# Starting every tile that the tensor engine reads at a multiple of 128 bytes in a two-layer decoder trunk

## The chip, the cores and the metric

The kernel runs as one program on one core of a Trainium2 chip. The metric is the device time of an execution in microseconds (us). Before the change it is 2058.88 us, the median of three runs (2056.41 to 2058.89).

## What is computed

Two decoder layers on 512 tokens of width 1024, all in float32. Layer 0 mixes tokens by attention (8 stick-breaking heads, 8 dilated heads), layer 1 by an mLSTM (8 heads). Each layer has a SwiGLU feed-forward network (FFN) of width 2816 ahead of its mixer and another behind it.

```python
def _rms_norm(x, g):
    y = x * lax.rsqrt(jnp.mean(x * x, axis=-1, keepdims=True) + EPS)
    return y * g

def _swiglu(x, w_gate, w_up, w_down):
    return (jax.nn.silu(x @ w_gate) * (x @ w_up)) @ w_down

for layer in range(2):
    x = x + 0.5 * _rms_norm(_swiglu(_rms_norm(x, g[0]), *ffn[layer, 0]), g[1])
    mix = attention(_rms_norm(x, g[2])) if layer == 0 else mlstm(_rms_norm(x, g[2]))
    x = x + _rms_norm(mix, g[3])
    x = x + 0.5 * _rms_norm(_swiglu(_rms_norm(x, g[4]), *ffn[layer, 1]), g[5])
```

## The kernel before

**Products in three passes.** A float32 operand is split into a high part (a cast to `fp32r`, `hi`) and a low part (the rest, `lo`), and a product is the sum of three matmuls: hi by hi, hi by lo, lo by hi (`mm3`, and the loops of `products`, `ffn` and `out_part`). All go through `mm` (L72), so the profile shows most matmuls under that one line, and they are told apart by their tiles. In a name such as `pg<-xnh,whi` the tile behind the arrow, `xnh`, is the moving operand, whose columns stream through the array, and the last one, `whi`, is the stationary operand, loaded into the array as weights beforehand (PEld in the profile).

**Stages.** Six run one after the other: FFN, attention, FFN, FFN, mLSTM, FFN. `proj` multiplies the normalized activations `xnh`/`xnl` (8 blocks of 128 features by 512 tokens) by 128 columns of a weight matrix: 8 blocks by three passes make 24 matmuls of 512 columns, or, at the start of a stage, where the tokens come in two halves, 48 of 256 columns. Weights come by DMA into `raw`, ACT casts them to `whi`, DVE (POOL for the first of a stage) subtracts to get `wlo` (`chunk`). The FFN's down-projection is a Strassen-like scheme: `left` and `right` form sums of activation and weight blocks, `hop` and `wop` split them into `hhi`/`hlo` (stationary) and `dhi`/`dlo` (moving, 512 columns), and `products` and the end of `ffn` accumulate into the banks `pc` and `po`. The mixers' `values` stream weights against stationary activations (`pv<-whi,xnh`, 256 columns), their heads multiply small tiles (`z`, `pv`, `nb`, `sb`), and `out_part` and `down` project the result (`po<-whi,mhi`, moving `whi`, stationary `mhi`/`mlo`).

**Order.** The order of the work is written in the program: a generator per head or token block gets its turn by an estimate of PE's clock (`clk`, `spawn`, `tick`). Each engine then runs its instructions in the order in which they were written.

**Where tiles start.** A pool lays its tiles out one behind the other in each partition, each rounded up to 32 bytes. `ident` starts at byte 2176 (17 times 128) and takes 512 bytes, `mhalf` (4 bytes, L52) takes 32, and so `x` and all that lies behind it start 32 bytes past a multiple of 128, until the next small tile shifts the rest again. In the built program the start, as the rest of a division by 128, is:

| tiles | read by PE as | start before | start after |
|---|---|---|---|
| `ident` | moving | 0 | 0 |
| `xnh`, `xnl` | moving in `pg`, `pq`, `ob`; stationary in `pv` | 32 | 0 |
| `whi`, `wlo` of the main pool | stationary in `pg`, `pq`, `ob`; moving in `pv`, `po` | 32 | 0 |
| `whi`, `wlo` of the pool `xp` (first 4 weight tiles of the second and the fourth FFN) | stationary in `pg` | 96 | 0 |
| `hhi`, `hlo`; `dhi`, `dlo` | stationary; moving, in `pc` and `po` | 64; 64 | 0; 0 |
| `mhi`, `mlo` | stationary in `po` | 64 | 0 |
| `tri` | stationary in `z` | 64 | 0 |
| heads' tiles (`ks`, `qq`, `ql`, `p5hi`, `p5lo`, `vt`, `qhi`, `khi`, `vhi`, `wshi`, `qshi`, `ones`, ...) | both, in `z`, `pv`, `nb`, `sb` | 96 | 0 |

The rows of `xnh` (2048 bytes per feature block), the 512 bytes of one weight block and the quarters of `hhi` are multiples of 128 bytes themselves, so every slice that PE reads starts at the same rest as its tile.

Of the kernel before, what the change touches and what calls it, by code (L numbers as in the profile page):

```python
# [10 lines left out]
F32 = mybir.dt.float32  # L11
# [5 lines left out]
P = 128  # L17
T = 512
D = 1024
KT = 8  # L20
TB = 4
# [21 lines left out]
class Trunk:  # L43
    def __init__(self, ctx, tc, a):
        self.ctx, self.tc, self.nc, self.a = ctx, tc, tc.nc, a
        nc = tc.nc
        self.cp = ctx.enter_context(tc.tile_pool(name="cp", bufs=1))
        self.pp = ctx.enter_context(tc.tile_pool(name="pp", bufs=1))
        self.ps = ctx.enter_context(tc.tile_pool(name="ps", bufs=8, space=PSUM))
        self.ident = self.cp.tile([P, P], F32, name="ident")  # L50
        make_identity(nc, self.ident)
        self.mhalf = self.cp.tile([P, 1], F32, name="mhalf")  # L52
        nc.gpsimd.memset(self.mhalf, -0.5)
        self.x = self.pp.tile([P, TB, D], F32, name="x")
        self.y = self.pp.tile([P, TB, D], F32, name="y")
        self.xnh = self.pp.tile([P, KT, T], F32R, name="xnh")
        self.xnl = self.pp.tile([P, KT, T], F32R, name="xnl")

        self.sums = self.pp.tile([P, TB, 2], F32, name="sums")
        self.qb = self.pp.tile([P, TB], mybir.dt.bfloat16, name="qb")  # L60
        self.qi = self.pp.tile([P, TB], F32, name="qi")
        self.qe = self.pp.tile([P, TB], F32, name="qe")

        self.clk, self.tasks, self.seq, self.busy = 0.0, [], 0, False
        self.xn_done = set()
        self.xpool = None
# [45 lines left out]
    def exp_ln(self):  # L112

        self.tc.keep_in_program_order(self.nc.scalar.preload_act_table_set("natural_log_exp_and_others"))


    def bank(self, name):
        return self.ps.tile([P, 512], F32, tag="ps", name=name)
# [87 lines left out]
    def rstd(self, src, f=1.0, eps=EPS, sums=None):  # L206

        nc = self.nc
        junk = self.pp.tile([P, 512], mybir.dt.bfloat16, tag="junk", bufs=1, name="junk")
        acc = eps  # L210
        for h in range(2):
            ss = self.pp.tile([P, 1], F32, tag="ss", bufs=4, name="ss") if sums is None else sums[:, h:h + 1]
            nc.scalar.activation(junk, src[:, h * 512:h * 512 + 512], AF.Square, accum_out=ss)  # L213
            v = self.pp.tile([P, 1], F32, tag="v", bufs=4, name="v")
            nc.vector.tensor_scalar(v, ss, f / D, acc, op0=ALU.mult, op1=ALU.add)
            acc = v
        r = self.pp.tile([P, 1], F32, tag="r", bufs=4, name="r")
        nc.gpsimd.tensor_tensor(r, v, self.mhalf, op=ALU.pow)  # L218
        return r

# [3 lines left out]
    def row_scales(self, fp):  # L224

        nc, v = self.nc, self.nc.vector
        q = self.pp.tile([P, TB], F32, tag="q", bufs=1, name="q")  # L230
        v.tensor_add(q, self.sums[:, :, 0], self.sums[:, :, 1])
        v.tensor_scalar(q, q, 1e-16 * EPS * D, None, op0=ALU.max)
        v.reciprocal(q, q)
        v.tensor_scalar(self.qb, q, EPS * D, 1.0, op0=ALU.mult, op1=ALU.add)
        v.tensor_copy(self.qi, self.qb)
        v.scalar_tensor_tensor(self.qe, self.qi, 4 * EPS, self.qi, op0=ALU.mult, op1=ALU.mult)
        t, = self.scratch(("xa",))
        b = self.bank("rs")
        for tb in range(TB):
            c = slice(tb * P, tb * P + P)  # L240
            nc.vector.tensor_scalar(t[:, c], self.ident, 0.0, self.qi[:, tb:tb + 1], op0=ALU.mult, op1=ALU.add)
            nc.tensor.transpose(b[:, c], t[:, c], self.ident)
            self.clk += 109
        self.rs = fp.tile([P, T], mybir.dt.bfloat16, name="rs")
        nc.scalar.copy(self.rs, b)
# [74 lines left out]
    def ffn(self, l, w, then, prefetch):  # L320
        nc, a = self.nc, self.a
        tc = self.tc
        with tc.tile_pool(name=f"ffn{l}{w}", bufs=1, reuse_waits="tile") as fp:
# [5 lines left out]
            for t in range(2):  # L329
                self.half(t)  # L330
                for i, (b, c) in enumerate(zip(bs, cs)):
# [2 lines left out]
                        self.row_scales(fp)  # L334
                    if t and i % 2:
                        hs.append(self.glu(fp, *bs[i - 1:i + 1]))
            if self.xpool:
                self.xpool.release()
                self.xpool = None
            with tc.tile_pool(name=f"dn{l}{w}", bufs=1, reuse_waits="tile") as dp:  # L340
                self.fp, self.dp = fp, dp
                todo = []
# [37 lines left out]
                n = len(ops)  # L380
# [111 lines left out]
    def attention(self, then, prefetch):  # L492
        nc, a, tc = self.nc, self.a, self.tc
        with tc.tile_pool(name="amix", bufs=1, reuse_waits="tile") as mp, \
                tc.tile_pool(name="dram", bufs=1, space=bass.MemoryType.DRAM) as dp:
            with tc.tile_pool(name="att", bufs=1, reuse_waits="tile") as ap:
                self.ap, self.p5 = ap, 2
                rest = self.attention_heads(ap, mp, dp)
            self.out_last(*rest, then, prefetch)

    def out_part(self, ws, mix, po, tb, ks):

        if tb not in po:
            po[tb] = [self.bank("po") for _ in range(2)]
        for h in range(2):
            for k in ks:
                st = [c[:, tb * P:(tb + 1) * P] for c in mix[k]]
                for (a, b) in ((0, 0), (0, 1), (1, 0)):
                    self.mm(po[tb][h], st[a], ws[k - 4][b][:, h * 512:(h + 1) * 512],
                            k == 4 and a == b, k == 7 and a == 1)  # L510
                self.tick()
# [233 lines left out]
    def toeplitz_rows(self, dp):  # L745


        nc, a, ap = self.nc, self.a, self.ap
        rb = ap.tile([32, 8], F32, name="rb")
        nc.sync.dma_start(rb, a["rel_bias"])  # L750
        oh = ap.tile([32, 640], F32, tag="f5", bufs=2, name="oh")
        nc.sync.dma_start(oh, a["onehot"])
        lm = ap.tile([8, 640], F32, tag="f5", bufs=2, name="lm")
        nc.sync.dma_start(lm, a["lnm"])
        yield W["tz"]
        for h in range(2):
            b = self.bank("tz")
            self.mm(b[:8, :320], rb, oh[:, h * 320:h * 320 + 320], True, True, f32=True)
            nc.vector.tensor_add(lm[:, h * 320:h * 320 + 320], lm[:, h * 320:h * 320 + 320], b[:8, :320])
        rows = dp.tile([8, 640], F32, name="rows")  # L760
        nc.sync.dma_start(rows, lm)
        self.tz = dp.tile([8, P * 641], F32, name="tz")
        nc.sync.dma_start(bass.AP(self.tz.tensor, self.tz.offset, [[P * 641, 8], [641, P], [1, 640]]),
                          bass.AP(rows.tensor, rows.offset, [[640, 8], [0, P], [1, 640]]))

    def dilated(self, ks, qq, ql, r, h):
        nc, ap = self.nc, self.ap
# [3 lines left out]
        bs = [self.bank("z") for _ in range(3)]  # L771
        lay = {3: (0, 0, 0), 2: (1, 0, 512), 0: (1, 384, 896), 1: (2, 0, 1024)}
        s = self.f5("s")
        mx = ap.tile([P, 4], F32, tag="mx", bufs=2, name="mx")
        ls = ap.tile([P, 4], F32, tag="ls", bufs=2, name="ls")
        for i, (b, c, f) in lay.items():
            n = (i + 1) * P
            q = slice(i * P, i * P + P)
# [3 lines left out]
        for i, (b, c, f) in lay.items():  # L782
            n = (i + 1) * P
# [3 lines left out]
        for i, (b, c, f) in lay.items():  # L787
            n = (i + 1) * P
# [3 lines left out]
        for i, (b, c, f) in lay.items():  # L792
            n = (i + 1) * P
# [25 lines left out]
    def mlstm_heads(self, ap, mp, dp):  # L819
            nc, a = self.nc, self.a  # L820
            self.cw = ap.tile([P, 16, 4], F32, name="cw")
            nc.sync.dma_start(self.cw, a["conv_w"])
            hg = ap.tile([P, KT], F32, name="hg")
            nc.sync.dma_start(hg, a["head_g"])
            onf = ap.tile([P, P], F32, tag="n2", bufs=1, name="onf")
            nc.gpsimd.memset(onf, 1.0 / P)
# [15 lines left out]
            rows = dp.tile([8, 1792], F32, name="rows")  # L842
# [127 lines left out]
    def gate_rows(self, gb, rows, ucol, ready):  # L970

        nc, a, ap = self.nc, self.a, self.ap
        bg = ap.tile([64, 1], F32, name="bg")
        nc.sync.dma_start(bg, a["b_gates"])
        st = ap.tile([P, 1792], F32, tag="bt", bufs=2, name="st")
        s0, s1 = st[:8, :T], st[:8, T:2 * T]
# [14 lines left out]
        b = f[0:8]  # L991
# [2 lines left out]
        nc.vector.scalar_tensor_tensor(ur, g[0:8], bg[0:8], b, op0=ALU.add, op1=ALU.subtract)  # L994
        mr = m[0:8]
        nc.vector.tensor_tensor_scan(mr, s1, ur, NEG, op0=ALU.add, op1=ALU.max)
        mp = ap.tile([8, 4], F32, name="mp")
        nc.vector.memset(mp, 0.0)
        gs = ap.tile([8, 4, 4], F32, name="gs")
        nc.vector.memset(gs, 0.0)  # L1000
        end = lambda t, c: t[:, c * P + P - 1:c * P + P]
        for c in range(3):
# [24 lines left out]
def build(tc, a, phases=("f00", "att", "f01", "f10", "mls", "f11")):  # L1027
    with ExitStack() as ctx:
        k = Trunk(ctx, tc, a)
# [19 lines left out]
        for n, (ph, l, gi, go) in enumerate(order):  # L1049
# [4 lines left out]
            gs = []  # L1054
# [14 lines left out]
                k.attention(then, prefetch)  # L1069
            else:  # L1070
                k.mlstm(then, prefetch)
        if k.xpool:
            k.xpool.release()


def pack(i):
# [61 lines left out]
```

## Time and profile before

| | |
|---|---|
| median of 3 runs | 2058.88 us |
| the profiled execution's own time | 2058.52 us |
| its span (first to last instruction) | 2056.8 us |
| PE busy | 1995.3 us, 97% |
| DVE, ACT, POOL busy | 64%, 46%, 25% |
| mean granted TensorE clock | 0.989 of full speed |
| HBM read | 196.65 MB |

How to read it: PE's busy time covers each stretch in which at least one matmul is in flight, and matmuls overlap, so a mean duration of a matmul (some 390 ns for 512 columns) says little. What the tensor engine takes for one more matmul is the distance between the starts of two neighbours, which the timeline shows.

### The profile page before, as it was taken

The numbers are of one execution on the slowest core, as the hardware profiler recorded it, in microseconds if no ns is written. First come the engines' busy times: TensorE is split into PE (matmuls) and PEld (weight loads), VectorE is DVE, ScalarE is ACT, GpSimd is POOL, SyncE is SP. The second block draws the span as 40 slices with busy tenths as digits, with TensorE's granted clock in tenths as the row PEclk, the third lists the DMA queues.
The fourth block names the chain that finished last, engine by engine and source line by source line (L and its number), as shares of the span: only waits on it lengthen the run. The fifth ranks groups of instructions, "written<-read, shape, count | busy, mean of one in ns | idle before, by whom it ended". The sixth has DMA issues, their size and how long they took to land. (4 is left out here: it accounts for less than half of the span.)

```text
span 2056.8 us, 25965 instructions
## 1 busy us (share of the span) xinstructions
PE 1995.3 (97%) x9876; PEld 1670.5 (81%) x9876; DVE 1319.6 (64%) x2016; ACT 955.8 (46%) x1649; POOL 504.0 (25%) x374
## 2 busy tenths in 40 slices
PE   8999999999997999999999999999999979999998
PEld 7888887888886978888788888888888868888887
DVE  6766554666578676665487566547776786675643
ACT  5443333477786353333244333325877654433321
POOL 4322302101004333220343232021010143332111
PEclk9999999999999999999999999999999999999999
DMA  5323332232122232333124323321433232333321
GB/s 184 123 94 105 99 113 72 86 114 69 57 72 83 91 125 92 103 104 111 53 82 133 104 92 102 112 67 52 157 103 109 89 100 89 127 93 112 104 83 41
DMA packets 56119, 200.51 MB, mean 97 GB/s; under 512 B 6521, under 2 KB 6649, under 8 KB 55994
## 3 DMA queue, kind: packets, MB, share of 16 engines
q1 hardware_dynamic: 55992, 198.85, 29.6%
q8 instruction: 77, 1.26, 0.3%
q14 instruction: 48, 0.39, 0.1%
q10 hardware_dynamic: 2, 0.00, 0.0%
HBM read 196.65 MB, written 4.80 MB: 98 GB/s over the span
## 5 line engine op out<-in xcount | busy, mean ns | idle before, releaser
L72 PE MATMUL pg<-xnl,whi 128*128 128x512 f32 (+1 forms) x1568 | 583.5, 372 | 6.1 <-DVE xnl L184 6.1
L72 PE MATMUL pg<-xnh,whi 128*128 128x512 f32 (+1 forms) x1568 | 583.7, 372 | 0.1
L72 PE MATMUL pg<-xnh,wlo 128*128 128x512 f32 (+1 forms) x1568 | 583.0, 372 | 0.0
L127 ACT CAST whi<-raw 128x1024 fp32r<-128x1024 f32 x248 | 259.3, 1049 | 455.0 <-issue 197.5
L128 DVE TENSOR_TENSOR wlo<-raw,whi 128x1024 fp32r<-128x1024 f32 x227 | 290.0, 1279 | 196.1 <-ACT whi L127 191.5
L72 PEld LDWEIGHTS pg<-xnl,whi 128*128 128x128 f32 x1568 | 296.6, 189 | 61.4 <-DVE xnl L184 6.8
L72 PEld LDWEIGHTS pg<-xnh,whi 128*128 128x128 f32 x1568 | 296.9, 189 | 55.0 <-ACT xnh L183 0.5
L72 PEld LDWEIGHTS pg<-xnh,wlo 128*128 128x128 f32 x1568 | 296.7, 189 | 54.7
L397 POOL TENSOR_TENSOR h<-h,rs 128x512 f32<-128x512 f32 x88 | 142.8, 1622 | 778.1 <-ACT h L396 750.4
L184 DVE TENSOR_TENSOR dlo<-raw,dhi 128x512 fp32r<-128x512 f32 x240 | 188.3, 804 | 91.1 <-ACT dhi L183 90.5
L183 ACT CAST dhi<-raw 128x512 fp32r<-128x512 f32 x240 | 146.5, 621 | 197.9 <-DMA raw<-down 152.2
L398 DVE TENSOR_TENSOR h<-h,pg 128x512 f32<-128x512 f32 x88 | 60.1, 683 | 224.7 <-PE pg L72 221.5
L72 PE MATMUL pc<-dhi,hhi 128*128 128x512 f32 x448 | 175.3, 391 | 3.9 <-ACT hhi L183 3.9
L72 PE MATMUL pc<-dhi,hlo 128*128 128x512 f32 x448 | 175.4, 392 | 0.6 <-DVE hlo L184 0.6
L72 PE MATMUL pc<-dlo,hhi 128*128 128x512 f32 x448 | 174.8, 390 | 0.0
L482 DVE TENSOR_TENSOR y<-y,pc 128x512 f32<-128x512 f32 x192 | 128.9, 678 | 5.6 <-PE pc L72 5.4
L72 PE MATMUL pq<-xnh,whi 128*128 128x512 f32 (+1 forms) x312 | 111.3, 358 | 0.5 <-DVE ql L634 0.5
L72 PE MATMUL pq<-xnl,whi 128*128 128x512 f32 (+1 forms) x312 | 111.0, 356 | 0.3 <-DVE xnl L184 0.3
L72 PE MATMUL pq<-xnh,wlo 128*128 128x512 f32 (+1 forms) x312 | 110.5, 355 | 0.0
L184 DVE TENSOR_TENSOR hlo<-h,hhi 128x256 fp32r<-128x256 f32 x208 | 103.3, 515 | 8.0 <-ACT hhi L183 7.8
L183 ACT CAST hhi<-h 128x256 fp32r<-128x256 f32 x208 | 78.9, 405 | 55.3 <-DVE h L398 48.6
L72 PEld LDWEIGHTS pc<-dhi,hhi 128*128 128x128 f32 x448 | 84.4, 188 | 22.5 <-ACT hhi L183 4.8
(237 smaller groups left out, 3322.3 us busy)
## 6 DMA issues: line engine op xcount, KB each, us to landing
raw<-gate SPq DMA_DIRECT2D x88, 512.0 KB, 3.5
raw<-up SPq DMA_DIRECT2D x88, 512.0 KB, 3.5
raw<-down SPq DMA_DIRECT2D x88, 512.0 KB, 3.5
raw<-mlstm_in SPq DMA_DIRECT2D x24, 512.0 KB, 3.5
raw<-attn_in SPq DMA_DIRECT2D x16, 512.0 KB, 3.4
bt<-rows SPq DMA_DIRECT2D x8, 896.0 KB, 4.3
gb<-norm_g SPq DMA_DIRECT2D x11, 512.0 KB, 4.1
raw<-attn_v SPq DMA_DIRECT2D x8, 512.0 KB
```

Source lines behind the costliest of these rows:

```text
L72: self.nc.tensor.matmul(out, lhsT=lhsT, rhs=rhs, start=start, stop=stop, skip_group_check=True)
L127: nc.scalar.copy(hi[:, :n], raw[:, :n])
L128: sub = (eng or nc.vector).tensor_sub(lo[:, :n], raw[:, :n], hi[:, :n])
L183: self.nc.scalar.copy(hi, src)
L184: self.nc.vector.tensor_sub(lo, src, hi)
L397: self.nc.gpsimd.tensor_mul(h, h, self.rs)
L398: self.nc.vector.tensor_mul(h, h, pu)
L482: self.nc.vector.tensor_add(dst, dst, b)
```

## The change

A helper `few` allocates a tile of a few columns with 128 bytes per partition (32 float32 or 64 bfloat16 elements) and returns the columns wanted. Every tile of a few columns is now made by it, which puts the tiles behind it at multiples of 128. The pool `xp`, which is laid against the other end of the memory, gets an unused tile of 24 float32 (96 bytes) ahead of its release. The core of the diff (the other fourteen tiles change as `mhalf` does):

```diff
-        self.mhalf = self.cp.tile([P, 1], F32, name="mhalf")
+        self.mhalf = self.few(self.cp, 1, "mhalf")
...
-        self.sums = self.pp.tile([P, TB, 2], F32, name="sums")
+        self.sums = self.few(self.pp, 2 * TB, "sums").rearrange("p (t s) -> p t s", t=TB)
...
+    def few(self, pool, n, name, bufs=1, dt=F32, rows=P):
+
+        return pool.tile([rows, 32 if dt is F32 else 64], dt, tag=name, bufs=bufs, name=name)[:, :n]
...
-            if self.xpool:
-                self.xpool.release()
-                self.xpool = None
+            self.end_xpool()
...
+    def end_xpool(self):
+        if self.xpool:
+            self.xpool.tile([P, 24], F32, name="pad")
+            self.xpool.release()
+            self.xpool = None
```

No instruction is added, removed or moved on any engine: the two programs have the same instructions in the same order. Six of them wait for another set of semaphores, since tiles of different pools now overlap a little differently: two casts `dhi<-raw` on ACT wait for one fewer, three subtractions `wlo<-raw,whi` on POOL for one or two more or fewer, one DMA `gb<-norm_g` on SP for one fewer.

## Rows read from the trace of the kernel before

**Rows 1.** The page's part 1: busy time, share of the span, instructions of each engine

```profile
PE 1995.3 (97%) x9876; PEld 1670.5 (81%) x9876; DVE 1319.6 (64%) x2016; ACT 955.8 (46%) x1649; POOL 504.0 (25%) x374
```

**Rows 2.** The page's part 2: PE's busy tenths and granted clock, 40 slices

```profile
PE   8999999999997999999999999999999979999998
...
PEclk9999999999999999999999999999999999999999
```

**Rows 3.** The waits of PE: us in total, times, longest us

```profile
PE pt L260 <- DVE xa L255: 20.2, 11, 7.5
PE pg L72 <- DVE xnl L184: 6.1, 3, 3.0
```

**Rows 4.** Groups of PE's instructions by form: xcount, then busy us, mean ns of one

```profile
L72 PE MATMUL pg<-xnh,whi 128*128 128x512 f32 x1248 | 492.2, 394 | 0.0
...
L72 PE MATMUL pc<-dhi,hhi 128*128 128x512 f32 x448 | 175.3, 391 | 3.9 <-ACT hhi L183 3.9
...
L72 PE MATMUL pg<-xnh,whi 128*128 128x256 f32 x320 | 91.5, 287 | 0.1
...
L72 PE MATMUL pq<-xnh,whi 128*128 128x512 f32 x200 | 79.6, 398 | 0.5 <-DVE ql L634 0.5
...
L72 PE MATMUL po<-dhi,hhi 128*128 128x512 f32 x192 | 76.2, 397 | 0.9 <-ACT hhi L183 0.9
...
L72 PE MATMUL pv<-whi,xnh 128*128 128x256 f32 x256 | 72.4, 283 | 0.9 <-DVE m L579 0.8
...
L72 PE MATMUL po<-whi,mhi 128*128 128x512 f32 x128 | 46.8, 407 | 0.1
...
L72 PE MATMUL pq<-xnh,whi 128*128 128x256 f32 x112 | 31.7, 285 | 0.0
...
L72 PE MATMUL ob<-xnh,whi 128*128 128x512 f32 x64 | 25.3, 395 | 0.0
...
L72 PE MATMUL z<-p5hi,tri 128*128 128x256 f32 x24 | 7.7, 321 | 0.0
```

**Rows 5.** PE's timeline, up-projection of one FFN tile: start us, us

```profile
300.01 0.40 PE L72 MATMUL pg<-xnh,whi 128*128 128x512 f32 x1
...
311.87 0.40 PE L72 MATMUL pg<-xnh,whi 128*128 128x512 f32 x1
```

**Rows 6.** PE's timeline, a long run of the down-projection

```profile
347.85 0.39 PE L72 MATMUL po<-dhi,hhi 128*128 128x512 f32 x1
...
356.91 0.39 PE L72 MATMUL po<-dlo,hhi 128*128 128x512 f32 x1
```

**Rows 7.** PE's timeline, attention's output projection, 512 columns

```profile
552.21 0.63 PE L72 MATMUL po<-whi,mhi 128*128 128x512 f32 x2
...
555.00 0.63 PE L72 MATMUL po<-whi,mhi 128*128 128x512 f32 x2
```

**Rows 8.** PE's timeline, first projections of the first FFN, 256 columns

```profile
27.85 0.28 PE L72 MATMUL pg<-xnh,whi 128*128 128x256 f32 x1
...
33.42 0.28 PE L72 MATMUL pg<-xnh,wlo 128*128 128x256 f32 x1
```

**Rows 9.** PE's timeline, first projections of the second FFN, 256 columns

```profile
671.00 0.28 PE L72 MATMUL pg<-xnh,wlo 128*128 128x256 f32 x1
...
673.84 0.28 PE L72 MATMUL pg<-xnh,whi 128*128 128x256 f32 x1
```

**Rows 10.** PE's timeline, attention's z products of 384 columns

```profile
423.58 0.53 PE L72 MATMUL z<-p5hi,tri 128*128 128x384 f32 x1
...
424.22 0.42 PE L72 MATMUL z<-p5hi,tri 128*128 128x256 f32 x1
```

**Rows 11.** The same stretch by engine: us, busy us of PE, PEld, DVE, ACT, POOL, clock, DMA

```profile
423.00:426.00 3.00, 3.00 (x13) 2.91 (x12) 2.01 (x4) 1.43 (x4) 0.80 (x2) 0.50 0.00 0
```

**Rows 12.** Groups of ACT's instructions by form

```profile
L183 ACT CAST dhi<-raw 128x512 fp32r<-128x512 f32 x240 | 146.5, 621 | 197.9 <-DMA raw<-down 152.2 <-PE pc L72 38.9 <-POOL raw L455 3.5
...
L183 ACT CAST qshi<-bt 128x512 fp32r<-128x512 f32 x8 | 5.0, 619 | 0.1
```

More of the change, by code (lines that the diff above doesn't have):

```diff
@@ L57, in __init__ @@
         self.xnl = self.pp.tile([P, KT, T], F32R, name="xnl")
-        self.sums = self.pp.tile([P, TB, 2], F32, name="sums")
-        self.qb = self.pp.tile([P, TB], mybir.dt.bfloat16, name="qb")
-        self.qi = self.pp.tile([P, TB], F32, name="qi")
-        self.qe = self.pp.tile([P, TB], F32, name="qe")
+        self.sums = self.few(self.pp, 2 * TB, "sums").rearrange("p (t s) -> p t s", t=TB)
+        self.qb = self.few(self.pp, TB, "qb", dt=mybir.dt.bfloat16)
+        self.qi = self.few(self.pp, TB, "qi")
+        self.qe = self.few(self.pp, TB, "qe")
         self.clk, self.tasks, self.seq, self.busy = 0.0, [], 0, False
@@ L211, in rstd @@
         for h in range(2):
-            ss = self.pp.tile([P, 1], F32, tag="ss", bufs=4, name="ss") if sums is None else sums[:, h:h + 1]
+            ss = self.few(self.pp, 1, "ss", 4) if sums is None else sums[:, h:h + 1]
             nc.scalar.activation(junk, src[:, h * 512:h * 512 + 512], AF.Square, accum_out=ss)
-            v = self.pp.tile([P, 1], F32, tag="v", bufs=4, name="v")
+            v = self.few(self.pp, 1, "v", 4)
             nc.vector.tensor_scalar(v, ss, f / D, acc, op0=ALU.mult, op1=ALU.add)
             acc = v
-        r = self.pp.tile([P, 1], F32, tag="r", bufs=4, name="r")
+        r = self.few(self.pp, 1, "r", 4)
         nc.gpsimd.tensor_tensor(r, v, self.mhalf, op=ALU.pow)
@@ L229, in row_scales @@
         nc, v = self.nc, self.nc.vector
-        q = self.pp.tile([P, TB], F32, tag="q", bufs=1, name="q")
+        q = self.few(self.pp, TB, "q")
         v.tensor_add(q, self.sums[:, :, 0], self.sums[:, :, 1])
@@ L748, in toeplitz_rows @@
         nc, a, ap = self.nc, self.a, self.ap
-        rb = ap.tile([32, 8], F32, name="rb")
+        rb = self.few(ap, 8, "rb", rows=32)
         nc.sync.dma_start(rb, a["rel_bias"])
@@ L773, in dilated @@
         s = self.f5("s")
-        mx = ap.tile([P, 4], F32, tag="mx", bufs=2, name="mx")
-        ls = ap.tile([P, 4], F32, tag="ls", bufs=2, name="ls")
+        mx = self.few(ap, 4, "mx", 2)
+        ls = self.few(ap, 4, "ls", 2)
         for i, (b, c, f) in lay.items():
@@ L822, in mlstm_heads @@
             nc.sync.dma_start(self.cw, a["conv_w"])
-            hg = ap.tile([P, KT], F32, name="hg")
+            hg = self.few(ap, KT, "hg")
             nc.sync.dma_start(hg, a["head_g"])
@@ L972, in gate_rows @@
         nc, a, ap = self.nc, self.a, self.ap
-        bg = ap.tile([64, 1], F32, name="bg")
+        bg = self.few(ap, 1, "bg", rows=64)
         nc.sync.dma_start(bg, a["b_gates"])
@@ L996, in gate_rows @@
         nc.vector.tensor_tensor_scan(mr, s1, ur, NEG, op0=ALU.add, op1=ALU.max)
-        mp = ap.tile([8, 4], F32, name="mp")
+        mp = self.few(ap, 4, "mp", rows=8)
         nc.vector.memset(mp, 0.0)
-        gs = ap.tile([8, 4, 4], F32, name="gs")
+        gs = self.few(ap, 16, "gs", rows=8).rearrange("p (a b) -> p a b", a=4)
         nc.vector.memset(gs, 0.0)
@@ L1071, in build @@
                 k.mlstm(then, prefetch)
-        if k.xpool:
-            k.xpool.release()
+        k.end_xpool()
 def pack(i):
```

## The prediction

> **What bounds the kernel now.** I read the busy times first: PE is busy 1995.3 us [rows 1] of a span of 2056.8, so all its idle time is 61.5 us, and no other engine passes 64%. The slices show this from end to end, with the clock granted at full speed nearly everywhere [rows 2]. The waits of PE are few and short; the largest kind, the transposes that wait for normalized activations, comes to 20.2 us in eleven times [rows 3]. Nothing but PE's own work can therefore give more than a few per cent, and the change does nothing but move tiles. So the question is whether the place of a tile sets how fast PE gets on, and that is read from the distances between starts on PE's timeline.
>
> The reader is to see five distances there. All are at the full clock unless said otherwise.
> - Projection, 512 columns, `xnh` moving and `whi` stationary, both starting at 32 past a multiple of 128: 51 steps from 300.01 to 311.87, 232.5 ns each [rows 5].
> - Down-projection, 512 columns, `dhi` and `hhi`, both at 64: 40 steps from 347.85 to 356.91, 226.5 ns each [rows 6].
> - Output projection, moving `whi` at 32, stationary `mhi` at 64: 12 steps from 552.21 to 555.00 (a row with x2 stands for two), 232.5 ns [rows 7].
> - Projection of 256 columns, both at 32: 47 steps from 27.85 to 33.42, 118.5 ns [rows 8].
> - The same of the second FFN, whose weights lie in `xp` at 96: 25 steps from 671.00 to 673.84, 113.6 ns [rows 9].
>
> The same size of matmul thus takes 6 ns less where its tiles start at 64, and 5 ns less in one case where the weights start elsewhere than the activations. The loss is about the same for 512 and for 256 columns: it is paid once per matmul, not per column. [...]
>
> **The change part by part.** *The starts.* All tiles that PE reads come to lie at 0. [...] I take 226.7, the step of tiles at 64 [rows 6] rounded up, since the loss differs between 32 and 64, which points to a boundary every 64 bytes, and 0 is on it too. The counts are from the groups [rows 4], times three for the three passes.
> - 512 columns: `pg` 3 x 1248, `pq` 3 x 200, `ob` 3 x 64 and the output projections 3 x 128 make 4920. Each gains 232.5 - 226.7 = 5.8 ns: 28.5 us.
> - 256 columns: `pv` 3 x 256, `pg` 3 x 320 less the 384 from `xp`, `pq` 3 x 112 make 1680. Each gains 118.5 - 113.6 = 4.9 ns: 8.2 us.
> - Head products with 256 columns or more (one row of some thirty stands in [rows 4]): some 460, at 5.3 ns between the two, 2.4 us. They stand among waits for the heads' own chains, so I count half: 1.2 us.
> - `pc` (3 x 448) and the FFN's `po` (3 x 192) already step at 226.5, and nothing is counted.
>
> That makes 37.9 us, all on the path, since PE is the engine that is never far ahead of a wait.
>
> *What waits take back.* A wait whose other side began with PE's own last product moves along with PE. One whose other side started earlier grows by what its cover shrinks: 38 us in 2057 is 1.8%, and with some 25 us of cover that is 0.45 us. If all of PE's waits, some twenty places of any size, were of that kind, they would take back 9 us; if none, 0. I take 3. Late next are the waits of [rows 3], not a new engine: DVE at 64% has room.
>
> *The other engines' operands.* They move too. ACT's cast of 512 columns takes 621 ns from `raw` at 32 into `dhi` at 64 and 619 ns from `bt` at 0 into `qshi` at 96 [rows 12]. I see no price of a start there and count nothing; PE's work covers it. The six changed waits are on ACT, POOL and SP, behind which weights are prepared ahead of PE; at 0.4 us a wait they would cost 2 us uncovered, and nothing as covered. The padding itself runs no instruction.
>
> *The sum.* The profiled execution takes 2058.5 us, 0.02% under the median. 2058.5 - 28.5 - 8.2 - 1.2 + 3 = **2023.6 us**, 1.7% faster.
>
> **The rivals.**
>
> *No change: the place decides, not the start.* `dhi`, `hhi` and the weights in `xp` lie in the upper part of the memory, `xnh` and `whi` in the lower one. If the loss comes from two reads in one region, the starts do nothing, and the time is 2058.5, give or take 4. For it: the 113.6 of [rows 9] is reached with `xnh` still at 32. Against it: `whi` with `mhi`, which lies higher, still steps at 232.5 [rows 7], and the upper `dhi` and `hhi` are both in one part and step well [rows 6]. [...]
>
> *Slower: operands with equal starts meet.* Today's dear steps of [rows 5, 8] have both operands at the same rest (32 and 32), and the cheap one of [rows 9] has them apart (32 and 96). If equal starts make the weight load and the stream of columns meet, then 0 and 0 would be dear everywhere, and the good cases would lose what they have now: 3 x 448 + 3 x 192 = 1920 at 5.8 ns is 11.1 us, the 384 of `xp` at 4.9 ns 1.9 us, so 2071.5 us. It decides against the kernel as soon as the step at 0 is above the mean of today's, (4920 x 232.5 + 1920 x 226.5) / 6840 = 230.8 ns. Against it: 64 and 64 is cheap [rows 6], and 32 with 64 is dear [rows 7].
>
> [...]
>
> **How the numbers follow.** The forecast has a chance of 0.83, no change 0.09, slower 0.05, much faster 0.03. A difference of up to 0.2% (4 us) can't be told from none, so faster is 0.83 + 0.03 = 0.86, same 0.09, slower 0.05. The forecast's own range: below, no wait takes anything back (3 us), the head products count in full (1 us), and the step at 0 is 2 ns under 226.7 (14 us): 2006. Above, the waits take 9 us and not 3, the 256-column steps gain only half (4 us), and the step at 0 is 1.5 ns above 226.7 (7 us): 2041. This leaves 0.17 outside, so it stands as the range.
>
> **What would show it.** In the profile of the changed kernel the steps of `pg`, `pq`, `ob` and the mixers' `po` should be 226.5 to 227 ns, as `pc` is, without the spread that makes 232.5 of them, and those of `pg`, `pq` and `pv` of 256 columns 113 to 114. `pc` and the `po` of the FFN should not change, which would refute the meeting of equal starts. PE should be busy near 1958 us, its idle time near 64. The prediction is wrong if the projections still step at 232 (no change), if `pc` steps at 232 (slower), if anything steps at 216 or less (much faster), or if the steps come out as said and PE's idle time grows by over 10 us.

## The result and the profile after

The changed kernel takes 2036.33 us (median of four runs, 2036.02 to 2038.15), the kernel before 2058.63 (four runs). The ratio is 0.9896, with a 95% interval from 0.9879 to 0.9913: 1.0% faster. The prediction was 2023.6 us, 1.7% faster, with a range from 2006 to 2041. Direction and range hold; the gain is 22 us and not 35. Two executions in what follows took far longer than the others of their kernel (3976.95 us of `a_w256`, 3281.56 of the kernel before) and are left out of the comparisons.

The page's part 1 (busy time, share of the span, instructions) and part 2 (busy tenths of PE and granted clock in 40 slices) of the changed kernel:

```profile
PE 1971.4 (97%) x9876; PEld 1668.0 (82%) x9876; DVE 1319.9 (65%) x2016; ACT 955.9 (47%) x1649; POOL 503.3 (25%) x374
...
PE   8999999999997999999999999999999989999998
...
PEclk9999999999998999999999999999999989999999
```

PE is busy 23.9 us less than before [rows 1]. The span is 2034.8 us instead of 2056.8, so PE's idle time grew from 61.5 to 63.4. The whole gain is thus in PE's own work, and waits took 2 us of it back. DVE, ACT and POOL are busy as long as before. The waits of PE (us in total, times, longest) answer to [rows 3] nearly unchanged:

```profile
PE pt L264 <- DVE xa L259: 20.4, 12, 7.4
...
PE pg L72 <- DVE xnl L188: 6.0, 3, 2.9
```

The groups of PE by form (xcount, then busy us and mean ns of one) answer to [rows 4]:

```profile
L72 PE MATMUL pg<-xnh,whi 128*128 128x512 f32 x1248 | 485.8, 389 | 0.0
...
L72 PE MATMUL pc<-dhi,hhi 128*128 128x512 f32 x448 | 176.1, 393 | 4.6 <-ACT hhi L187 4.6
...
L72 PE MATMUL pg<-xnh,whi 128*128 128x256 f32 x320 | 91.2, 286 | 0.1
...
L72 PE MATMUL pq<-xnh,whi 128*128 128x512 f32 x200 | 78.4, 392 | 0.7 <-DVE ql L642 0.7
...
L72 PE MATMUL po<-whi,mhi 128*128 128x512 f32 x128 | 46.8, 407 | 0.1
```

`pg` and `pq` of 512 columns came down (492.2 to 485.8 and 79.6 to 78.4). The mixers' `po` did not move at all: 46.8 us and 407 ns, to the digit. The timeline (start us, us) shows why, in four stretches of neighbouring matmuls that answer to [rows 5, 7, 8, 9]:

```profile
28.06 0.28 PE L72 MATMUL pg<-xnh,whi 128*128 128x256 f32 x1
...
33.46 0.28 PE L72 MATMUL pg<-xnh,whi 128*128 128x256 f32 x1
...
295.74 0.39 PE L72 MATMUL pg<-xnl,whi 128*128 128x512 f32 x1
...
311.84 0.39 PE L72 MATMUL pg<-xnh,whi 128*128 128x512 f32 x1
...
552.83 0.62 PE L72 MATMUL po<-whi,mlo 128*128 128x512 f32 x2
...
558.40 0.62 PE L72 MATMUL po<-whi,mlo 128*128 128x512 f32 x2
...
664.11 0.28 PE L72 MATMUL pg<-xnl,whi 128*128 128x256 f32 x1
...
667.91 0.28 PE L72 MATMUL pg<-xnh,whi 128*128 128x256 f32 x1
```

- Projection of 512 columns: 16.10 us over 71 steps, 226.8 ns. It was 232.5. This is the forecast.
- The mixers' output projection: 5.57 us over 24 steps, 232.1 ns. It was 232.5, and 226.7 was forecast.
- Projection of 256 columns in the first FFN: 5.40 us over 45 steps, 120.0 ns. It was 118.5, and 113 to 114 was forecast: it got slower.
- The same in the second FFN with weights from `xp`: 3.80 us over 32 steps, 118.8 ns. It was 113.6: 5 ns lost.

All these tiles start at a multiple of 128 now, and the steps still differ. So the start of a tile does not set the step.

**A second theory.** It came from the addresses in the two built programs. Take the start of the weights minus the start of the moving tile, and of that the rest of a division by 256 bytes; this text calls it the distance. (The table of starts ahead of the prediction fixes it up to 128 bytes; which half it is in comes from the programs, and the steps of group 3 agree.) The padding moved `xnh` by 96 bytes and `whi` by 1248, and with that their distance from 128 to 0. `dhi` and `hhi` were at 0 before and stayed there. The mixers' `po` went from 160 to 128, and the products from `xp` from 64 to 128. If 512 columns are cheap at distance 0 and dear elsewhere, and 256 columns cheap at 64 and dearest at 0, all four readings follow, and the starts need no price of their own.

### The profile page after: what moved, and what is told of

It is laid out like the page before. It is cut to its first block, busy times and chain, and to the rows that moved or that the text cites. A ratio compares the mean times of both kernels' runs of the same rounds, so it can differ in the third digit from the quotient of the medians.

```text
span 2034.8 us, 25965 instructions
## 1 busy us (share of the span) xinstructions
PE 1971.4 (97%) x9876; PEld 1668.0 (82%) x9876; DVE 1319.9 (65%) x2016; ACT 955.9 (47%) x1649; POOL 503.3 (25%) x374
## 4 chain that ended last, share of the span: by engine, by line
PE 72%; DVE 8%; issue 8%; ACT 6%; POOL 4%; DMA 1%; SPq 0%; POOLq 0%; DVEq 0%; ACTq 0%
PE pg L72 40%; PE pc L72 14%; PE pq L72 5%; PE po L72 4%; PE pv L72 4%; PE ob L72 2%; DVE x L289 2%; PE z L72 1%; POOL r L222 1%; DVE dlo L188 1%; DVE xa L259 1%; POOL yg L283 1%; DVE xnl L188 1%; POOL wlo L132 1%; POOL h L399 1%
## 5 line engine op out<-in xcount | busy, mean ns | idle before, releaser
L72 PE MATMUL pg<-xnl,whi 128*128 128x512 f32 (+1 forms) x1568 | 576.5, 368 | 6.0 <-DVE xnl L188 6.0
L72 PE MATMUL pg<-xnh,whi 128*128 128x512 f32 (+1 forms) x1568 | 577.0, 368 | 0.1
L72 PE MATMUL pg<-xnh,wlo 128*128 128x512 f32 (+1 forms) x1568 | 576.5, 368 | 0.0
```

The costliest lines, as they stand in the source:

```text
L72: self.nc.tensor.matmul(out, lhsT=lhsT, rhs=rhs, start=start, stop=stop, skip_group_check=True)
```

## The experiments

Twelve runs were made. In groups 1, 2 and 4 the step means come from all neighbouring starts of a kind in the timeline that lie within 25 ns of the cheap step (so without waits and stretches at half the clock; "undisturbed" below). All kernels but the one of group 3 have the same 9876 matmuls in the same order, so two traces are compared step by step.

**1. The distance or the start.** One edit, made once in the kernel before and once in the changed one: 128 unused bytes ahead of the weight tiles of the main pool, and 128 behind them, so that only `whi` and `wlo` move against the rest (what lies behind them moves by 256).

```diff
     def chunk(self, src, n=1024, pool=None, tag="w", bufs=4, eng=None):
...
+        first = pool is self.pp and not self.shifted
+        if first:
+            self.shifted = True
+            pool.tile([P, 32], F32, name="ahead")
         hi = pool.tile([P, 1024], F32R, tag=tag + "hi", bufs=bufs, name="whi")
         lo = pool.tile([P, 1024], F32R, tag=tag + "lo", bufs=bufs, name="wlo")
+        if first and 32:
+            pool.tile([P, 32], F32, name="behind")
```

In the kernel before (`b_w128`), the starts of `xnh` and `whi` stay 32 past a multiple of 128, and the distance of the projections goes from 128 to 0:

> The kernel before, with 128 bytes put ahead of the weight tiles and 128 behind them, so that only whi and wlo of the main pool move, from 32 to 32 past a multiple of 128: no tile gains a better start. Distance theory (the loss goes by the distance between the start of the weights and that of the moving tile, as the rest of a division by 256): pg, pq and ob of 512 columns come to distance 0 and step at 227 ns instead of 232.5; the 256-column steps go from 118.5 to 120. 4536 x 5.6 ns = 25 us less, 1680 x 1.5 = 2.5 us more, waits take back 1 to 2: about 2037 us. Start theory (multiples of 64 or 128 bytes are fast): nothing changes, 2058 to 2059 us.

In the changed kernel (`a_w128`), all starts stay multiples of 128, and the distance goes from 0 back to 128:

> The changed kernel, with whi and wlo of the main pool alone moved by 128 bytes: all tiles still start at multiples of 128. Distance theory: pg, pq and ob are back at distance 128 and at 232.4 ns, 25 us more; po of the mixers comes to distance 0, 227 ns, 2 us less; 256 columns at 118.5 instead of 120, 2.5 us less: about 2056 us. Start theory: nothing changes, about 2036 us.

`b_w128` took 2041.04 us against 2058.13 of the kernel before in the same session, ratio 0.9915 [0.9900, 0.9929]. `a_w128` took 2063.27, ratio 1.0024 [1.0014, 1.0033]. Part 1 of the page and PE's timeline in the same FFN tile as above, first of `b_w128`:

```profile
PE 1975.3 (97%) x9876; PEld 1668.0 (82%) x9876; DVE 1320.0 (65%) x2016; ACT 955.5 (47%) x1649; POOL 504.0 (25%) x374
```

```profile
295.79 0.39 PE L72 MATMUL pg<-xnh,whi 128*128 128x512 f32 x1
...
311.88 0.39 PE L72 MATMUL pg<-xnh,wlo 128*128 128x512 f32 x1
```

and of `a_w128`:

```profile
PE 1997.4 (97%) x9876; PEld 1668.1 (81%) x9876; DVE 1320.3 (64%) x2016; ACT 956.8 (46%) x1649; POOL 503.6 (24%) x374
```

```profile
298.22 0.40 PE L72 MATMUL pg<-xnh,whi 128*128 128x512 f32 x1
...
311.98 0.39 PE L72 MATMUL pg<-xnh,wlo 128*128 128x512 f32 x1
```

16.09 us over 71 steps is 226.6 ns with both tiles off the multiples of 128. 13.76 us over 59 steps is 233.2 ns with both on them. So 256 bytes of padding, put in one place, give most of what the whole change gives (17 of 22 us), and the change with its weights moved by 128 gives nothing and loses 5 us. The starts are refuted as the cause, the distance stands. Its own times were less exact: both kernels came out dearer than it said, by 4 us (2037) and 7 us (2056). A part of the 7 us is that the dear steps of `a_w128` are 233.2 ns and not 232.4; the rest was not traced.

**2. Other distances, and the period.** The same edit in the changed kernel with 64, 192 and 256 bytes ahead of the weights (and 192, 64 and none behind).

> The changed kernel, with whi and wlo of the main pool alone moved by 64 bytes. Distance theory: pg and pq of 256 columns come to distance 64, as the weights in xp had before, and step at 113.6 instead of 120, 928 x 6.3 ns = 6 us less; pv, where the roles are exchanged, comes to distance 192, not seen so far; 512 columns at distance 64 were not seen either, between 227 and 233: 2030 to 2056 us. Start theory at 64: nothing changes, 2036 us. Start theory at 128: the weights' start is lost, pg back at 232, 2056 us, and 256 columns not faster than 118.5.

> The changed kernel, with whi and wlo of the main pool alone moved by 192 bytes. Distance theory: pv of 256 columns comes to distance 64 and steps at 113.6 instead of 120, 768 x 6.4 ns = 5 us less; pg and pq come to distance 192, not seen so far, 227 to 233 for 512 columns: 2031 to 2058 us. Start theory: as for 64 bytes, 2036 (multiples of 64) or 2056 us (multiples of 128), and pv like pg in its steps.

> The changed kernel, with whi and wlo of the main pool alone moved by 256 bytes. Distance theory with a period of 256 bytes: every distance is as in the changed kernel, pg, pq and ob of 512 columns at 227 ns, 256 columns at 120, 2036 us. If the period is 512 bytes: pg, pq and ob lose again, some 232 ns, 2055 to 2063 us.

`a_w64` took 2063.59 us (ratio 1.0026 [1.0017, 1.0036]), `a_w192` 2045.40 (0.9933 [0.9917, 0.9948]), `a_w256` 2037.32 (0.9892 [0.9876, 0.9909]; the kernel before took 2059.91 in its session). `a_w64` lies above the 2030 to 2056 that were expected: 512 columns at distance 64 take 233.4 ns, more than the 227 to 233 assumed. The steps of `a_w256` were read from one more run:

> The kernel of a_w256 once more for its profile. Period of 256 bytes: pg, pq and ob of 512 columns at 227 ns, 256 columns at 120, about 2037 us. Period of 512 bytes: 232 ns.

That run took 2039.11 us with steps of 226.8 (512 columns), 119.9 (256 columns) and 232.4 (mixers' `po`), as the changed kernel has them. A shift of 256 bytes changes nothing, so the period is 256 bytes or a divisor of it; 128 and 64 are excluded by group 1 and `a_w64`. The step means in ns, the distance in brackets:

| kernel | `pg`, 512 | mixers' `po`, 512 | `pg`, 256 | `pg` from `xp`, 256 | `pv`, 256 |
|---|---|---|---|---|---|
| before | 232.3 (128) | 233.5 (160) | 118.6 (128) | 114.3 (64) | 118.9 (128) |
| after | 226.8 (0) | 232.4 (128) | 119.9 (0) | 118.6 (128) | 119.8 (0) |
| `b_w128` | 227.1 (0) | 233.2 (32) | 119.9 (0) | 115.7 (64) | 119.8 (0) |
| `a_w128` | 233.2 (128) | 228.0 (0) | 119.0 (128) | 118.8 (128) | 118.8 (128) |
| `a_w64` | 233.4 (64) | 233.4 (64) | 116.1 (64) | 119.2 (128) | 116.5 (192) |
| `a_w192` | 228.9 (192) | 229.6 (192) | 117.0 (192) | 118.7 (128) | 114.9 (64) |

Each column follows its own distance and not the kernel: in `a_w128` `pg` gets dear and the mixers' `po` cheap by the same edit. 512 columns want 0, and 256 columns want 64 and do worst at 0 in this table.

**3. A stream without the kernel.** 24 matmuls of each case, from one moving tile and one weight tile (eight blocks of it by turns, 512 bytes apart) and nothing else, with weights that start 16 bytes further in each case (`fulla` to `fullp` with 512 columns, `halfa` to `halfp` with 256). In `off` the moving tile starts 32 bytes further and the weights with it. In `nearw` and `farw` the weights alternate between distance 0 and 128.

```diff
+        def mm(b, n, d, m=0):
+            j = count[0] % 8
+            count[0] += 1
+            o = j * P + (d + 4 * m) % 256 // 4
+            nc.tensor.matmul(b[:, :n], lhsT=wts[:, o:o + P], rhs=mov[:, m:m + n], start=True, stop=True,
+                             skip_group_check=True)
```

> Leaves out the whole computation and returns its input: only matmuls from one moving tile and one weight tile, 24 with each distance between their starts, both tiles based at the same rest of 256 bytes. fulla to fullp: 512 columns at distance 0, 16, 32, ... 240 bytes; halfa to halfp: 256 columns at the same; offa, offe, offi, offm: 512 columns at distance 0, 64, 128, 192 with the moving tile's start moved by 32 bytes; nearw and farw: weights at distance 0 and 128 by turns. Distance theory: steps of 512 columns 227 ns at 0, 233 to 235 at 32 and 64, 228 at 96, 232 to 233 at 128, 229 to 230 at 192, 235 at 224; of 256 columns 120 at 0, 115 to 116 at 64, 118.7 at 128, 117 at 192; off like full; by turns, the step in which the weights at 128 are loaded (behind a nearw) is dear and the other cheap. Start theory: off is dear at every distance, full cheap at 0, 64, 128 and 192 alike. If it is something of the kernel (writes by other engines, regions of the memory), nothing differs here.

It ran in 197.03 us. Rows of PE's timeline; each stands for 24 matmuls, so the step is the difference to the next start, divided by 24 (good to 0.4 ns, as the rows have 0.01 us):

```profile
26.13 5.60 PE L1055 MATMUL fulla<-mov,wts 128*128 128x512 f32 x24
31.57 5.61 PE L1055 MATMUL fullb<-mov,wts 128*128 128x512 f32 x24
37.02 5.75 PE L1055 MATMUL fullc<-mov,wts 128*128 128x512 f32 x24
...
59.36 5.77 PE L1055 MATMUL fullg<-mov,wts 128*128 128x512 f32 x24
64.97 5.76 PE L1055 MATMUL fullh<-mov,wts 128*128 128x512 f32 x24
...
109.58 5.62 PE L1055 MATMUL fullp<-mov,wts 128*128 128x512 f32 x24
115.03 3.03 PE L1055 MATMUL halfa<-mov,wts 128*128 128x256 f32 x24
117.91 3.01 PE L1055 MATMUL halfb<-mov,wts 128*128 128x256 f32 x24
...
126.42 2.89 PE L1055 MATMUL halfe<-mov,wts 128*128 128x256 f32 x24
129.14 3.01 PE L1055 MATMUL halff<-mov,wts 128*128 128x256 f32 x24
```

`fulla` (0) takes 226.7 ns, `fullb` (16) 227.1, `fullg` (96) 233.8, `fullp` (240) 227.1. All sixteen, from the same view, in ns:

| distance | 0 | 16 | 32 | 48 | 64 | 80 | 96 | 112 | 128 | 144 | 160 | 176 | 192 | 208 | 224 | 240 |
|---|---|---|---|---|---|---|---|---|---|---|---|---|---|---|---|---|
| 512 columns | 226.7 | 227.1 | 232.9 | 233.3 | 232.9 | 231.7 | 233.8 | 233.3 | 233.3 | 233.8 | 232.9 | 229.6 | 229.2 | 232.9 | 233.8 | 227.1 |
| 256 columns | 120.0 | 118.3 | 118.3 | 117.9 | 113.3 | 118.8 | 117.5 | 120.0 | 120.0 | 117.9 | 120.0 | 117.9 | 117.9 | 116.7 | 116.7 | 119.6 |

So the dependence needs no other engine: DVE, ACT and POOL do nothing in this stretch (us, then busy us of PE, PEld, DVE, ACT, POOL, clock, DMA):

```profile
26.00:182.60 156.60, 156.60 (x867) 135.69 (x865) 0.00 (x0) 0.00 (x0) 0.00 (x0) 1.00 0.00 1
```

512 columns have one good place, 0 and 16 bytes on either side, a half-good one at 176 to 192, and lose 5 to 7 ns elsewhere. 256 columns have one narrow good place, 64; 0 is among their worst, with 112, 128 and 160. 96 bytes was a miss: 228 was expected and 233.8 measured. With the moving tile moved by 32 bytes the cases at 64, 128 and 192 took 233.3, 232.5 and 229.6, as without; the one at 0 took 229.2 (`offa`, 5.50 us over 24 steps), where `fulla` took 226.7. The alternation was a miss too: 233.3 ns behind `nearw`, 230.9 behind `farw`, where one of the two should have been cheap (more on it below).

**4. The rest of the gain.** Three kernels from the changed one. `a_mix` moves only the mixers' `mhi` and `mlo`, so that `po` gets distance 0:

```diff
+            mp.tile([P, 32], F32, name="ahead")
```

> The changed kernel, with 128 unused bytes ahead of the pool of mhi and mlo in both mixers, so that these stand at distance 0 from whi. Distance theory: po of the mixers goes from 232.4 to 227 ns, 341 undisturbed steps x 5.3 ns = 2 us less, about 2034 us. Start theory: all tiles start at multiples of 128 as before, no step changes, 2036 us.

`a_off` makes the weight tiles 64 columns wider and starts those of the 256-column products 16 columns in (48 in `xp` and for `values`), so that these come to distance 64:

```diff
-        hi = pool.tile([P, 1024], F32R, tag=tag + "hi", bufs=bufs, name="whi")
+        hi = pool.tile([P, 1088], F32R, tag=tag + "hi", bufs=bufs, name="whi")[:, off:off + 1024]
...
+                                          off=48 if pool else 16) if n else
...
-            w = self.chunk(src[n, c])
+            w = self.chunk(src[n, c], off=48)
```

> The changed kernel, with weight tiles 256 bytes longer; the weights of the 256-column products (the first ones of a stage, and those of values) lie 64 or 192 bytes into their tile, which puts them at distance 64 from the activations, all others at 0. Distance theory: 256-column steps of pg, pq and pv go from 120 to 115 or 116 ns, 943 + 360 + 765 steps x 4.5 ns = 9 us less, 512 columns stay at 227: about 2027 us. Start theory at 64 bytes: no change, 2036 us; at 128 bytes: the 256-column steps get no better than 118.5 to 120.

`best` is both, with 128 unused bytes ahead of the FFN's tiles too, so that going from the projection to the down-projection and back keeps distance 0:

> The two edits before together, and 128 unused bytes ahead of the FFN's tiles too, so that hhi and dhi stand at distance 0 from xnh and whi where pg and pc follow each other. Distance theory: 9 us for the 256-column steps, 2 us for po of the mixers, 132 changes between pg and pc at 5.8 ns, 0.8 us: about 2025 us. Start theory: 2036 us.

| kernel | median us | ratio to before | PE busy us |
|---|---|---|---|
| `a_mix` | 2038.21 | 0.9892 [0.9877, 0.9907] | 1972.9 |
| `a_off` | 2036.27 | 0.9885 [0.9870, 0.9899] | 1968.3 |
| `best` | 2034.18 | 0.9874 [0.9857, 0.9890] | 1965.9 |

The steps moved as the distance says. The mixers' `po` of `a_mix`, on the timeline, takes 4.08 us over 18 steps, 226.7 ns (228.1 in the mean), where the changed kernel had 232.1:

```profile
555.35 0.61 PE L72 MATMUL po<-whi,mlo 128*128 128x512 f32 x2
...
559.43 0.62 PE L72 MATMUL po<-whi,mlo 128*128 128x512 f32 x2
```

In `a_off` the 256-column products take 113.4 ns in the best stretch (below, 665.43 to 670.42, 44 steps) and 116.2, 115.8 and 114.6 (`pg`, `pv`, `pq`) in the mean. But the times did not follow. `a_mix` was to save 2 us and can't be told from the changed kernel. `a_off` was expected at 2027 and gave nothing that can be told either. Step by step against the changed kernel, those undisturbed in both are 7.5 us shorter in `a_off`, and all the others (beside a wait, or at half the clock) together 6.6 us longer; the span is 2033.9 us against 2034.8. One such place is the start of the second FFN. PE's timeline of the changed kernel, a wait and the last matmul of the tile behind it, then the clock there (windows: us, busy us of PE, PEld, DVE, ACT, POOL, clock, DMA):

```profile
659.31 0.39 PE L72 MATMUL pg<-xnl,whi 128*128 128x256 f32 x1 [2.75 <-DVE xnl L188]
...
662.02 0.28 PE L72 MATMUL pg<-xnh,wlo 128*128 128x256 f32 x1
```

```profile
661.70:662.20 0.50, 0.50 (x6) 0.40 (x4) 0.50 (x1) 0.00 (x0) 0.00 (x0) 1.00 0.00 0
```

and the same in `a_off`:

```profile
659.29 0.38 PE L72 MATMUL pg<-xnl,whi 128*128 128x256 f32 x1 [2.84 <-DVE xnl L189]
...
663.01 0.41 PE L72 MATMUL pg<-xnh,wlo 128*128 128x256 f32 x1
...
665.43 0.28 PE L72 MATMUL pg<-xnh,wlo 128*128 128x256 f32 x1
...
670.42 0.28 PE L72 MATMUL pg<-xnl,whi 128*128 128x256 f32 x1
```

```profile
661.70:663.20 1.50, 1.50 (x9) 1.50 (x8) 1.50 (x4) 0.00 (x0) 0.00 (x0) 0.50 0.00 0
```

The wait is 0.09 us longer in `a_off`, and after it the clock falls to 0.50 in the middle of the tile, where the changed kernel keeps 1.00. The tile ends 0.99 us later, though its first steps are shorter. But the traces do not show that the edit brought this about. In `a_w256_look`, whose steps are those of the changed kernel, the clock falls in the same place:

```profile
663.12 0.39 PE L72 MATMUL pg<-xnl,whi 128*128 128x256 f32 x1 [2.84 <-DVE xnl L194]
```

```profile
665.50:667.00 1.50, 1.50 (x8) 1.50 (x8) 1.50 (x4) 0.00 (x0) 0.00 (x0) 0.50 0.00 0
```

In `best_again` (group 5), which has `a_off`'s edits in it, it stays, behind a longer wait:

```profile
658.32 0.39 PE L72 MATMUL pg<-xnl,whi 128*128 128x256 f32 x1 [2.86 <-DVE xnl L189]
```

```profile
660.70:661.20 0.50, 0.50 (x6) 0.39 (x4) 0.50 (x1) 0.00 (x0) 0.00 (x0) 1.00 0.00 0
```

`best`, the same kernel, was at 0.50 there, behind 2.88 us. So neither the shorter steps nor the length of the wait settles whether the clock falls there. `a_w256_look` also shows how much such places matter without any change of a step: PE is busy 1975.4 us in it at a mean clock of 0.987, against 1971.4 at 0.990 in the changed kernel. A saving of 2 us, as in `a_mix`, can't be seen beside that, and what took back the 6.6 us of `a_off` stays open.

**5. Once more, side by side.** The changed kernel and `best` in one session, five rounds:

> The changed kernel once more, on the same chip as best_again, to compare the two: 2036 to 2038 us.

> The kernel of best once more beside the changed kernel. Distance theory: its steps of 256 columns and of the mixers' po are cheaper by some 11 us in sum, of which waits and half-clock stretches took most back in the first look: 2 to 4 us under the changed kernel. If the first difference was chance: no difference.

2038.13 us (0.9907 [0.9893, 0.9921]) and 2035.35 (0.9890 [0.9876, 0.9904]), with the kernel before at 2058.1. Side by side `best` was ahead by 2.8 us, within the 2 to 4 expected, and its first runs had a lower ratio too (0.9874 against 0.9896 of the changed kernel in another session). But the intervals overlap: a likely small gain, not a proven one. The first time `best` was expected at 2025, and that was wrong.

**Which weights count.** While a matmul streams, the weights of the next one are loaded. In the changed kernel's timeline (PE and PEld), the load for the matmul that starts at 311.84 runs beside the one that starts at 311.61:

```profile
311.61 0.39 PE L72 MATMUL pg<-xnh,wlo 128*128 128x512 f32 x1
311.61 0.19 PEld L72 LDWEIGHTS pg<-xnh,whi 128*128 128x128 f32 x1
311.84 0.39 PE L72 MATMUL pg<-xnh,whi 128*128 128x512 f32 x1
```

Where a projection ends and a down-projection begins, the two differ: in the changed kernel each tile is at distance 0 to its own weights, and at 128 to those of the neighbour. PE's timeline of the changed kernel over 552 steps with 16 such changes:

```profile
132.76 0.39 PE L72 MATMUL pc<-dhi,hhi 128*128 128x512 f32 x1
...
258.04 0.39 PE L72 MATMUL pc<-dhi,hhi 128*128 128x512 f32 x1
```

and of `best`, where these distances are 0 too:

```profile
132.35 0.39 PE L72 MATMUL pc<-dhi,hhi 128*128 128x512 f32 x1
...
257.47 0.39 PE L72 MATMUL pc<-dhi,hhi 128*128 128x512 f32 x1
```

125.28 against 125.12 us: `best` steps at 226.7 ns throughout, and the changed kernel loses 0.16 us, 10 ns at each change. In the changed kernel the steps onto the other tile take 232.5 ns and the ones behind them 230.8, in the mean of the undisturbed changes, where `best` has 226.7 and 226.8. Each matmul has distance 0 to its own weights, so those don't explain it; it speaks for the next load as the one that counts, with a loss that trails into the next step. The alternation of group 3 fits that: 233.3 ns where the weights at 128 are loaded, 230.9 in the step behind. It remains an argument, since other pairs of tiles (the two streams, the two weight tiles) are 128 apart at these changes too.

## Why the prediction was right and wrong

- **What bounds the kernel**: held. The time fell by what PE's busy time fell (23.9 us), less 1.9 us of idle time. No other engine became the bound. PE's busy time was to be near 1958 us and is 1971.4.
- **512 columns, `pg`, `pq` and `ob`** (26.3 of the 28.5 us): held in size. The steps are 226.8, 227.4 and 227.9 ns where 226.7 was taken, and the 4418 that are undisturbed in both traces come to 24.1 us less. But the reason given was not the cause.
- **512 columns, the mixers' `po`** (3 x 128 at 5.8 ns, 2.2 us): failed. 233.5 became 232.4, since the distance went from 160 to 128: 0.4 us.
- **256 columns** (8.2 us gained): failed in sign. 118.5 became 120.0, and the products from `xp` went from 113.6 to 118.8. The 1995 steps undisturbed in both traces come to 3.3 us more, so this term alone is 11.5 us off, where the whole forecast is 12.7 us off; the smaller errors of the other terms cancel in part.
- **Head products** (1.2 us gained): failed, too small to matter; the 177 steps of 256 columns or more that are undisturbed in both traces come to 0.2 us less.
- **`pc` and the FFN's `po`**: unchanged, as said (226.9 and 227.1 ns).
- **What waits take back** (3 us): held, at 1.9.
- **Other engines, padding, changed waits**: held at nothing; the busy times of ACT, DVE and POOL agree within 1 us.
- **The range**: its lower end counts 2 ns on 6840 steps, its upper end 1.5 ns on 4920 only; on 6840 the upper end would be 2044 us and not 2041. The measured time lies inside either way.

**The step that failed** is "since the loss differs between 32 and 64, which points to a boundary every 64 bytes, and 0 is on it too". It read a cause off one start, when each row has two: that of the stream and that of the weights. The rows held a counterexample: starts of 32 and 96, neither of them on a boundary of 64 bytes, were cheap at 256 columns, and the prediction took that very step as what a start at 0 would give. What the runs showed in its place is the distance between the two starts: 226.8 ns at 0 and 233.2 at 128 with both tiles at multiples of 128 (the changed kernel and `a_w128`). The places of the tiles beyond a multiple of 128, which the built program tells, would have shown distances of 64, 160, 128 and 0. With 512 columns cheap only at 0 the forecast would have left out the mixers' `po`, and for 256 columns at 0 it had no row at all: it took the 113.6 ns of tiles at 32 and 96, and 120.0 came.

That the time fell inside the range is in good part luck. The change was made for the starts, and brought the distance of the projections from 128 to 0 as a side effect. `a_w128` fulfils the prediction's condition just as well, with all tiles at multiples of 128, and takes 2063.27 us, 0.2% more than the kernel before.

Of the rivals, "the place decides, not the start" had the right family and the wrong form: places decide, but by their difference in each 256 bytes, and the padding changed that. Moving the weights of the main pool by 128 bytes, with all starts still at multiples of 128, costs 27 us (`a_w128` against the changed kernel), and the distance is worth up to 7 ns a matmul of 512 columns in group 3. "Operands with equal starts meet" is false for 512 columns (226.7 ns at 0); 256 columns are dear at 0 (120.0 ns), but as dear at 112, 128 and 160.

**Still open.** Why the distance matters is not settled. That the weights' load and the stream collide is argued from the changes between projection and down-projection; no run took the load away. Nor does anything here say why 256 columns want another distance than 512. "Much faster" never came near: its mark of 216 ns or less was the author's estimate, no run shows such a step, and the best runs of 512 columns step at 226.6 ns. Two steps of 384 columns take 0.64 us at a clock of 0.50 [rows 10, 11]; scaled to 512 columns and a clock of 1.00 that is 213 ns a step, an estimate too. The mean steps of every start and distance tried stayed above it. And where the 6.6 us of `a_off` went, and what decides whether the clock falls behind a wait, was not varied on purpose.

## What to carry to other kernels

When two sizes of step show up for matmuls of one shape, tabulate for each the place of the moving tile and of the weights loaded beside it, and their difference, before blaming alignment: here the difference in 256 bytes decided, and 256 bytes of padding in one place gave 17 of the 22 us that padding every tile gave. The good difference depends on the number of columns (0 for 512, with 226.7 ns, and 64 for 256, with 113.3 ns, in group 3), so one layout does not serve both. And a saving of a few ns in steps around waits may not arrive: of 7.5 us saved in the undisturbed steps of `a_off`, 0.9 was left in the span. Where the half-clock stretches fall differs between runs of the same kernel (at the start of the second FFN 0.50 in `best` and 1.00 in `best_again`), so such savings are to be compared step by step.

## What was not expected of the hardware

- The step depends on the distance between weights and stream: 226.7 ns at 0 and 231.7 to 233.8 at most others with 512 columns, 113.3 at 64 and 120.0 at 0 with 256 columns.
- Distance 0, the best for 512 columns (226.7 ns), is among the worst for 256 (120.0 ns; the sixteen distances take 113.3 to 120.0).
- One distance does not always give one step: 512 columns at 0 took 226.7 ns in the mean of `fulla` and 229.2 in that of `offa`, and 256 columns at 64 took 113.4 ns in one stretch of `a_off` and 116.2 in its mean.
- In the same place behind a wait of 2.84 us the clock fell to 0.50 (`a_off`, `a_w256_look`), in `a_off` at a price of 1.0 us against the changed kernel, and behind one of 2.86 us it stayed at 1.00 (`best_again`).
